# A hybrid attention block in fp32r on one core: the rooms of weights moved 64 bytes up in SBUF

## The chip, the core and the metric

The kernel runs on one core of one Trainium2 chip. The metric is the device time of one execution in microseconds; of several runs the median is given. A profile is one further execution, recorded by the hardware profiler. Its span reaches from the first to the last recorded instruction; the time of a run holds a few microseconds more around it.

## What is computed

One layer of a decoder block over 512 tokens and 16 learned meta tokens (L = 528), width 1024, in float32:

```python
u = rmsnorm(h, pre_norm_g)                      # h: 528 x 1024
proj = u @ w_in                                 # 1024 x 7600
cq, ckv, k_pe, z_mla, fq, fk, fv, f, z_fox, gate_a, gate_b = split(proj)
q = (rmsnorm(cq) @ w_uq)                        # 16 heads, 64 plain + 32 rotary columns
k_nope, v_mla = (rmsnorm(ckv) @ w_ukv)
o_mla = causal_attention(q, k, v_mla)
o_fox = causal_attention(fq, fk, fv, cum=cumsum(log_sigmoid(f + b)))
y_mla = (o_mla * silu(z_mla)) @ w_br_mla
y_fox = (o_fox * silu(z_fox)) @ w_br_fox
mixed = (sigmoid(gate_a) * y_mla + sigmoid(gate_b) * y_fox) @ w_out
out = (h + rmsnorm(mixed, post_norm_g))[16:]
```

## The kernel before

Every product is made of matmuls of 128 rows by 128 columns of weights against up to 512 columns of tokens. To keep float32's precision each operand is split into a high and a low part (tile names ending in h and l), and a product is three matmuls: high by high, high by low, low by high. So one unit of work, 128 output columns of `w_in`, is 8 blocks of the inner dimension times 3, that is 24 matmuls, all issued by `mm` (line 98).

**Where the operands lie.** A matmul has a stationary operand, which is loaded into the array ahead of it (the profile's PEld, one load for each matmul), and a moving operand, which streams through. In `unit` (matmuls from `mm`, line 98) the weights are stationary and the tokens are moving. The rooms are:
- `uTh`, `uTl`: the normalised tokens, 8 blocks of 576 columns (2304 bytes) each. The meta tokens stand in columns 48 to 63 of a block and the real tokens from column 64 on, so that real tokens begin at a multiple of 256 bytes.
- the pool `wp`, three rooms each of `wraw` (weights as they come from DRAM), `wh` and `wl` (their high and low parts), 4096 bytes a room. At the start its `wraw` rooms also hold three tiles of x.
- `cTh`, `cTl`: the latent tokens, three blocks of 528 columns (2112 bytes).
- in the last stage `gh`, `gl` (the gated attention outputs), `a1h`, `a1l`, `a2h`, `a2l` (sums and halves of the merged branches) and again the rooms of `uTh`, `uTl`, reused for sums.

**The stages.** First the tokens are normalised and turned, with the small projections (`psm`). Then come 16 stages of attention, FoX and MLA in turn for each of 8 pairs of heads; each has its scores (`st`) and its values (`ov`), and between them, to fill the wait for softmax, the units of the next stage: `fq`, `fk`, `v`, `z` against `uTh`/`uTl`, and `mq`, `mk`, `v` and `ppe` against `cTh`/`cTl`. A product over all 528 tokens (`fk`, `v`, `mk`) is cut into 272 columns, which begin at the meta tokens, and 256 columns. Then the gates (`pg`) and the two branch products follow: one by a fast scheme of seven half products over 256 columns for each of four pairs of blocks (`pair_py`: tiles `x`, `y`, `z`), the other plainly (`py`, 512 columns). Last comes `w_out`, where the weights move and the tokens are stationary (`x`, `y`, `z` again).

**What sets the order.** PE's order is the order of the code (`manual_schedule`). ScalarE makes `wh` from `wraw` (line 131), GpSimd or VectorE makes `wl` (line 104). All DMAs are issued by SyncE's queue. The loads of the next three units are issued when a unit begins (`ahead`), and each waits until its `wraw` room is free.

**What sets the addresses.** A pool takes its rooms from the bottom of SBUF upward in the order in which pools and tiles are opened, or, with side="right", from the top downward. `const`, with `ident`, `eps_t`, `uTh` and `uTl`, lies at the bottom, `wp` follows it, and what is opened later lies above `wp`: in the attention `cqk` (with `cTh`, `cTl`) and the rest, in the last stage, when `cqk` is closed, `gh`, `gl` and others directly above `wp`. `a1h` to `a2l`, `tb`, `gT` and `th` lie on the right side.

Of the kernel before, what the change touches and what calls it, by code (L numbers as in the profile page):

```python
# [11 lines left out]
F32 = mybir.dt.float32  # L12
# [43 lines left out]
def block_kernel(ctx: ExitStack, tc: tile.TileContext, x, meta_tokens, pre_norm_g, w_in, fox_forget_b,  # L56
# [11 lines left out]
    const = ctx.enter_context(tc.tile_pool(name="const", bufs=1))  # L68
# [6 lines left out]
    nc.gpsimd.memset(eps_t[:, 1:2], 4.0 * EPS)  # L75
    uT0 = [const.tile([128, KD, ROW + L - META], F32R, tag=n, name=n) for n in ("uTh", "uTl")]
    uTh, uTl = (t[:, :, ROW - META :] for t in uT0)
    padp = ctx.enter_context(tc.tile_pool(name="padp", bufs=1, side="right"))
    pad = padp.tile([128, 56], F32, tag="pad", name="pad")

# [84 lines left out]
    thp = ctx.enter_context(tc.tile_pool(name="thp", bufs=5, side="right"))  # L165
    cctx = ExitStack()
    cqk = cctx.enter_context(tc.tile_pool(name="cqk", bufs=1))
    cTh = cqk.tile([128, 3, L], F32R, tag="cTh", name="cTh")
    cTl = cqk.tile([128, 3, L], F32R, tag="cTl", name="cTl")
    accp = ctx.enter_context(tc.tile_pool(name="accp", bufs=3, space=PSUM))  # L170
# [1223 lines left out]
```

## Time and profile before

| | us |
|---|---|
| three runs: median (lowest, highest) | 587.31 (587.02, 587.46) |
| span of the profiled execution | 584.6 |
| PE busy | 575.7 (98%) |
| PEld, the loads of stationary operands | 496.8 (85%) |
| VectorE busy | 416.4 (71%) |
| ScalarE busy | 357.4 (61%) |
| GpSimd busy | 199.4 (34%) |
| DMA, share of 16 engines | 70.3% |

The profile gives no time of its own for the profiled execution beside its span. The span lies 2.7 us below the median of the runs, which is what lies around it if that execution was an average one.

How to read it: a PE busy time of 98% says only that matmuls overlap without a gap, since a matmul's record reaches from its start to its modelled end, and the next one starts long before that. How fast PE really goes is read from the distance between the starts of two matmuls, called the pitch here: in the chain of work that ended last a piece "5.44 PE z L98 x24" means that 24 matmuls took 5.44 us from the first start to the start of what followed, a pitch of 226.7 ns. In a group's row the second number behind the bar is the mean record of one matmul, so two groups of the same width with records 7 ns apart have pitches about 7 ns apart.

### The profile page before, as it was taken

To read this page: it belongs to the slowest core of one execution; us is meant where nothing else is said; L and a number is where in the kernel's file an instruction comes from. 1 tells how busy PE (TensorE), PEld (TensorE's weight loads), DVE (VectorE), ACT (ScalarE), POOL (GpSimd) and SP (SyncE) were. 2 spreads that over 40 slices of the span, in tenths; PEclk is the share of its full clock that TensorE was granted. 3 is DMA by queue.
4 is the path that set the end of the run, shared out by engine and by line. 5 is a ranking of instruction groups with operands and counts; after the bars stand their busy time and mean duration, and the time that the engine had idled before them with its cause. 6 is when DMAs were issued, how large, how long until landed. Compare 5 with 4: busy or idle time off the path is not lost.

```text
span 584.6 us, 11115 instructions
## 1 busy us (share of the span) xinstructions
PE 575.7 (98%) x3841; PEld 496.8 (85%) x3841; DVE 416.4 (71%) x1156; ACT 357.4 (61%) x816; POOL 199.4 (34%) x270
## 2 busy tenths in 40 slices
PE   8999999999999999999999999999999999999996
PEld 6989889889889888888898898878998998888884
DVE  5854877885776775767758748896647876468966
ACT  7856774893774775767748747944343462443762
POOL 4317745464468462654554634510000000000000
PEclk9999999999999999999999999999999999999998
DMA  8535599989977999988986976977722534233503
GB/s 295 122 83 163 127 176 230 231 195 248 177 167 158 228 191 206 219 172 207 183 176 180 219 154 147 183 172 236 233 73 72 145 104 144 78 109 108 217 0 144
DMA packets 220000, 97.47 MB, mean 167 GB/s; under 512 B 131456, under 2 KB 209672, under 8 KB 219944
## 3 DMA queue, kind: packets, MB, share of 16 engines
q1 hardware_dynamic: 219944, 96.77, 70.3%
q8 instruction: 30, 0.49, 0.3%
q14 instruction: 26, 0.21, 0.1%
HBM read 62.36 MB, written 3.97 MB: 113 GB/s over the span
## 4 chain that ended last, share of the span: by engine, by line
PE 96%; ACT 1%; DMA 1%; issue 0%; SPq 0%; DVE 0%; POOL 0%; DVEq 0%; ACTq 0%; POOLq 0%
PE z L98 19%; PE pg L98 15%; PE v L98 9%; PE fk L98 8%; PE st L98 8%; PE fq L98 8%; PE x L98 8%; PE py L98 7%; PE ov L98 5%; PE psm L98 3%; PE y L98 2%; PE mq L98 2%; PE mk L98 1%; PE ppe L98 1%; DMA wsr<-in_w_in_dram 1%; ACT uTh L371 0%
## 5 line engine op out<-in xcount | busy, mean ns | idle before, releaser
L104 POOL TENSOR_TENSOR wl<-wraw,wh 128x1024 fp32r<-128x1024 f32 (+2 forms) x61 | 118.3, 1947 | 112.2 <-ACT wh L131 80.5
L131 ACT CAST wh<-wraw 128x1024 fp32r<-128x1024 f32 (+1 forms) x72 | 74.6, 1042 | 56.4 <-PE py L98 16.8
L826 ACT ACTIVATE sf<-sf,nb 128x272 f32<-128x272 f32 (+3 forms) x128 | 72.7, 569 | 11.5 <-DVE nb L791 10.6
L865 DVE SCALAR_TENSOR_TENSOR pn<-sf,ri,pn 128x512 f16<-128x512 f32 (+3 forms) x128 | 69.6, 609 | 1.6 <-ACT pn L861 1.5
L104 DVE TENSOR_TENSOR wl<-wraw,wh 128x512 fp32r<-128x512 f32 (+1 forms) x55 | 52.2, 950 | 23.9 <-ACT wh L1119 17.8
L861 ACT ACTIVATE pn<-sf,ri 128x128 f16<-128x128 f32 (+3 forms) x128 | 59.7, 548 | 0.5 <-DVE ri L831 0.5
L98 PE MATMUL z<-uTh,wh 128*128 128x512 f32 x128 | 50.9, 398 | 0.0
L98 PE MATMUL pg<-uTh,wh 128*128 128x512 f32 x128 | 50.2, 392 | 0.0
L98 PE MATMUL z<-uTl,wh 128*128 128x512 f32 x128 | 50.1, 391 | 0.0
L98 PE MATMUL z<-uTh,wl 128*128 128x512 f32 x128 | 50.0, 390 | 0.0
L98 PE MATMUL pg<-uTl,wh 128*128 128x512 f32 x128 | 49.9, 390 | 0.0
L98 PE MATMUL pg<-uTh,wl 128*128 128x512 f32 x128 | 49.8, 389 | 0.0
L706 DVE TENSOR_REDUCE vsc<-v 128x1 f32<-128x272 f32 (+1 forms) x32 | 13.2, 433 | 39.8 <-PE v L98 39.8
L98 PE MATMUL st<-hlk,hlq 64*128 64x272 f32 (+4 forms) x480 | 41.3, 299 | 0.0
L1119 ACT CAST wh<-wraw 128x512 fp32r<-128x512 f32 x28 | 17.3, 618 | 37.9 <-DVE wraw L1128 17.0
L98 PE MATMUL v<-uTh,wl 128*128 128x256 f32 (+1 forms) x128 | 36.5, 285 | 0.0
L98 PE MATMUL fk<-uTl,wh 128*128 128x256 f32 (+1 forms) x128 | 36.4, 285 | 0.0
L98 PEld LDWEIGHTS st<-hlk,hlq 64*128 64x128 f32 x480 | 33.0, 186 | 4.1 <-ACT vh L725 2.8
L98 PE MATMUL fk<-uTh,wh 128*128 128x256 f32 (+1 forms) x128 | 36.4, 285 | 0.0
L98 PE MATMUL v<-uTl,wh 128*128 128x256 f32 (+1 forms) x128 | 36.4, 285 | 0.0
L98 PE MATMUL fk<-uTh,wl 128*128 128x256 f32 (+1 forms) x128 | 36.4, 285 | 0.0
L98 PE MATMUL v<-uTh,wh 128*128 128x256 f32 (+1 forms) x128 | 36.4, 284 | 0.0
(295 smaller groups left out, 1612.3 us busy)
## 6 DMA issues: line engine op xcount, KB each, us to landing
wraw<-in_w_in_dram SPq DMA_DIRECT2D x56, 512.0 KB, 4.8
cbp<-c_dram SPq DMA_DIRECT2D x16, 264.0 KB, 4.1
wraw<-in_w_br_fox_dram SPq DMA_DIRECT2D x8, 512.0 KB, 4.5
tb<-in_w_out_dram SPq DMA_DIRECT2D x8, 512.0 KB, 5.4
wraw<-in_w_br_mla_dram SPq DMA_DIRECT2D x8, 512.0 KB, 4.3
wraw<-in_w_out_dram SPq DMA_DIRECT2D x6, 512.0 KB, 3.6
xr<-in_x_dram SPq DMA_DIRECT2D x4, 512.0 KB
out_dram<-yo SPq DMA_DIRECT2D x8, 256.0 KB, 2.0
```

Source lines behind the costliest of these rows:

```text
L98: nc.tensor.matmul(*a, **k)
L104: return eng.tensor_tensor(out=lo, in0=src, in1=f32(hi), op=ALU.subtract)
L131: nc.scalar.copy(wh[:, :n], raw[:, :n])
L706: nc.vector.tensor_reduce(out=sc[:, i : i + 1], in_=ps, op=ALU.max, axis=AX.X, apply_absolute_value=True)
L826: exps[b // 3] = nc.scalar.activation(sf, sf, AF.Exp, bias=sums["nb"][:, h, b : b + 1], scale=-1.0, accum_out=sums["su"][:, h, b : b + 1]).ins
L861: normed[:] = [nc.scalar.activation(hi, sf, AF.Copy, scale=rib).ins]
L865: nc.vector.scalar_tensor_tensor(out=lo, in0=sf, scalar=rib, in1=hi, op0=ALU.mult, op1=ALU.subtract)
L1119: nc.scalar.copy(to[0], src)
```

## The change

Two tiles that nothing reads or writes are put between the others. The first is 16 float32 (64 bytes for each partition) at the end of `const`; it moves all that lies above it on that side by 64 bytes. The second is 48 float32 (192 bytes) at the start of `cqk`; it moves `cTh`, `cTl` and what is opened behind them by 192 bytes more, 256 in all.

```diff
@@ -75,6 +75,7 @@
     uT0 = [const.tile([128, KD, ROW + L - META], F32R, tag=n, name=n) for n in ("uTh", "uTl")]
     uTh, uTl = (t[:, :, ROW - META :] for t in uT0)
+    const.tile([128, 16], F32, tag="shift", name="shift")
     padp = ctx.enter_context(tc.tile_pool(name="padp", bufs=1, side="right"))
@@ -165,6 +166,7 @@
     cctx = ExitStack()
     cqk = cctx.enter_context(tc.tile_pool(name="cqk", bufs=1))
+    cqk.tile([128, 48], F32, tag="shift", name="shift2")
     cTh = cqk.tile([128, 3, L], F32R, tag="cTh", name="cTh")
```

The instructions, their order on each engine and their waits are the same in both kernels; only addresses differ. They are, for the first byte of each room:

| room | before | after | modulo 256 before, after |
|---|---|---|---|
| `uTh`, `uTl` (real tokens begin 256 bytes later) | 17152, 35584 | the same | 0, 0 |
| `wraw`, three rooms | 54016, 58112, 62208 | +64 | 0, 64 |
| `wh`, three rooms | 66304, 70400, 74496 | +64 | 0, 64 |
| `wl`, three rooms | 78592, 82688, 86784 | +64 | 0, 64 |
| `cTh`, `cTl` and all else of the attention on this side | 90880, 97216 | +256 | unchanged |
| `gh`, `gl`, and in the last stage also `thx`, `yo`, `xr`, `gp` | 90880, 107264 | +64 | 0, 64 |
| `a1h`, `a1l`, `a2h`, `a2l`, `tb` | 161216, 165312, 169408, 177600, from 128448 on | the same | 192, 192 |

A block of weights is 128 columns, 512 bytes, so all blocks of a `wh` room share the room's remainder. What matmuls meet, as remainders modulo 256 of the moving and the stationary operand's first byte:

| matmuls | count | columns | before | after |
|---|---|---|---|---|
| `z`, `pg`, `fq` against `uTh`, `uTl` | 960 | 512 | 0, 0 | 0, 64 |
| `fk`, `v`, second part | 384 | 256 | 0, 0 | 0, 64 |
| `fk`, `v`, first part (begins at the meta tokens) | 384 | 272 | 192, 0 | 192, 64 |
| `py` (512 columns), and `x`, `y`, `z` of `pair_py` against `gh`, `gl` (256) | 192 + 192 | 512, 256 | 0, 0 | 64, 64 |
| `x`, `z` of `pair_py` against `a1h` to `a2l` | 144 | 256 | 192, 0 | 192, 64 |
| `w_out`, `x` and `z` with the rooms of `uTh`, `uTl` stationary | 96 | 512 | 0, 0 | 64, 0 |
| `w_out`, `x` and `y` with `a1h` to `a2l` stationary | 48 | 512 | 0, 192 | 64, 192 |
| `mq`, `ppe`, `mk`, MLA's `v` against `cTh`, `cTl` | 168 | 512, 272, 256 | 0 to 192, 0 | 0 to 192, 64 |
| scores, values, `psm`, transposes, the last 24 of `w_out` | the rest | | unchanged | unchanged |

## The prediction

> **What bounds the kernel now.** I read the page first: busy shares, clock and the chain that ended last.
>
> ```profile
> span 584.6 us, 11115 instructions
> PE 575.7 (98%) x3841; PEld 496.8 (85%) x3841; DVE 416.4 (71%) x1156; ACT 357.4 (61%) x816; POOL 199.4 (34%) x270
> PEclk9999999999999999999999999999999999999998
> PE 96%; ACT 1%; DMA 1%; issue 0%; SPq 0%; DVE 0%; POOL 0%; DVEq 0%; ACTq 0%; POOLq 0%
> ```
>
> PE holds 96% of the chain, at full clock. No weights are waited for in the body: DMA's 1% is one load at the start. So the time is the number of matmuls times their pitch, and since the change adds, removes and moves no instruction, only a change of pitch, or a weight load that becomes late, can reach the end. I went on to the chain in order of time, which gives pitches of stretches without a wait.
>
> ```profile
> 430.78 1.44 PE z L98 x12
> 436.40 1.36 PE z L98 x12
> 546.02 5.49 PE y L98 x24
> 551.51 5.44 PE z L98 x24
> ```
>
> The columns are start, length, what, and how many matmuls. The first two are twelve matmuls of 256 columns each, in the same scheme: 1.44/12 = 120.0 ns against 1.36/12 = 113.3 ns. They differ in the moving operand alone: `gh` and `gl` (remainder 0 modulo 256) in the first, `a2h` and `a2l` (192) in the second, with weights at 0 in both. The last two are 24 of 512 columns in `w_out`: 5.49/24 = 228.8 ns with stationary `a2h`, `a2l` (192), 5.44/24 = 226.7 ns with the rooms of `uTh`, `uTl` (0), moving weights at 0 in both. So **the place of the operands modulo 256 goes with the pitch**, by up to 6.7 ns a matmul, and in both directions. I call "distance" the stationary remainder less the moving one, modulo 256: 0 gives 120.0 and 226.7, 64 gives 113.3, 192 gives 228.8. That distance and not the two places decides is an assumption; the rows don't hold all pairs of places.
>
> [...]
>
> **The change part by part.** 1. *Long matmuls against the tokens*: `z`, `pg`, `fq`, from places 0, 0 to 0, 64.
>
> ```profile
> L98 PE MATMUL z<-uTh,wh 128*128 128x512 f32 x128 | 50.9, 398 | 0.0
> L98 PE MATMUL pg<-uTh,wh 128*128 128x512 f32 x128 | 50.2, 392 | 0.0
> L98 PE MATMUL fq<-uTh,wh 128*128 128x512 f32 x64 | 25.9, 405 | 0.0
> 174.17 2.80 PE ppe L98 x12
> 497.00 5.44 PE pg L98 x24
> 567.83 10.99 PE x L98 x48
> ```
>
> Each of these three groups has two sisters (tokens low, weights low) of the same count: 3 x (128 + 128 + 64) = 960 matmuls, at 5.44/24 = 226.7 ns in an undisturbed stretch of `pg`. The trace shows no long matmul at distance 64. The long ones at mixed or other distances are `y` above (228.8), `ppe` (2.80/12 = 233.3, latent tokens at 0, 64 and 128) and the last 48 `x` (10.99/48 = 229.0; half of them run at 0, half with `a2h`, `a2l`). None of these is under 226.7, so for 512 columns the present place looks like the floor. I take the mean of the three rows, (5.49 + 10.99 + 2.80)/84 = 229.5 ns: 960 x (229.5 - 226.7) = **+2.7 us**. Ends: 233.3 gives 960 x 6.6 = +6.3; nothing excludes that distance 64 helps here as it does at 256 columns, 960 x (-6.7) = -6.4.
>
> 2. *Second parts of `fk` and `v`*, 256 columns, from 0, 0 to 0, 64.
>
> ```profile
> L98 PE MATMUL fk<-uTh,wh 128*128 128x256 f32 x64 | 18.1, 283 | 0.0
> L98 PE MATMUL z<-a2h,wh 128*128 128x256 f32 x16 | 4.4, 276 | 0.0
> L98 PE MATMUL mk<-cTl,wh 128*128 128x256 f32 x8 | 2.3, 283 | 0.0
> ```
>
> Six such groups of 64 (two tensors, three passes) are 384 matmuls at a record of 283 ns, that is 120.0 ns of pitch. At distance 64 stands the second row, 276 ns, or 113.3 of pitch. I take it: 384 x (-6.7) = **-2.6 us**. Ends: -2.6, and 0 if places count and not the distance; a loss is bounded by the step from `z` to `mk` in the other direction, +2.6.
>
> 3. *First parts of `fk` and `v`*, 272 columns, distance 64 to 128.
>
> ```profile
> L98 PE MATMUL fk<-uTh,wl 128*128 128x272 f32 x64 | 18.3, 287 | 0.0
> L98 PE MATMUL v<-cTh,wl 128*128 128x272 f32 x8 | 2.3, 288 | 0.0
> L98 PE MATMUL mk<-cTl,wh 128*128 128x272 f32 x8 | 2.4, 294 | 0.0
> ```
>
> Again 384. `cTh`'s third block begins at remainder 128, so the second row has distance 128: 1 ns more, **+0.4 us**. Ends: 0, and the third row's +7 ns, +2.7.
>
> 4. *`pair_py` against `a1h` to `a2l`*, 144 of 256 columns, distance 64 to 128. `mk` with `cTl` in part 2's rows has distance 128 and 283 ns against 276: 144 x 6.7 = **+1.0 us**, ends 0 and +1.0.
>
> 5. *`py` and `pair_py` against `gh`, `gl`*: both operands move, distance stays 0, so **0**. Upper end by the pair of rows with both at 192 against both at 0:
>
> ```profile
> L98 PE MATMUL x<-a1h,a2h 128*128 128x512 f32 x4 | 1.6, 394 | 0.0
> L98 PE MATMUL py<-gh,wh 128*128 128x512 f32 x64 | 24.9, 389 | 0.0
> ```
>
> 5 ns for 384 matmuls, +1.9; a gain of the size of part 2 would be 192 x 6.7 = -1.3.
>
> 6. *`w_out`*: 96 go from distance 0 to 192, at 228.8 instead of 226.7: **+0.2 us**; 48 go from 192 to 128, taken as 0; ends -0.3 and +0.9 (233.3 for all 144). *Latent tokens*, 168: their distances are permuted, **0**, ends 168 x 3 ns = 0.5 to either side.
>
> 7. *The DMAs and the other engines* work on rooms 64 bytes higher.
>
> ```profile
> GB/s 224 331 297 341 399 405 405 405 397 389 328 347 316 302 248 31 6 3 151 345 172 162 334 143 0 0 0 0 0 0 0 0 0 0 0 20 177 333 213 290
> GB/s 0 0 0 0 0 0 0 0 0 0 0 37 53 328 406 225 33 37 369 393 213 4 0 0 0 0 57 29 328 406 225 4 0 139 279 229 205 279 385 410
> wraw<-in_w_in_dram SPq DMA_DIRECT2D x56, 512.0 KB, 4.8
> L131 ACT CAST wh<-wraw 128x1024 fp32r<-128x1024 f32 x70 | 73.5, 1053 | 56.4 <-PE py L98 16.8 <-PE v L98 11.7 <-PE z L98 7.2
> L131 ACT CAST wh<-tb 128x1024 fp32r<-128x1024 f32 x6 | 6.3, 1045 | 1.7 <-PE z L98 1.2 <-PE x L98 0.5
> ```
>
> The first row is the window 404 to 436 us, where `w_out` is loaded into `tb` at remainder 192; the second is 525 to 545 us, the same rows of 2048 bytes into `wraw` at 0. Both reach about 405 GB/s, so the remainder costs those DMAs nothing. ScalarE's cast takes 1045 ns from `tb` and 1053 from `wraw`. I cost all this at **0**; the cover is the load's lead: 4.8 us from issue to landing for weights that 24 matmuls of 226.7 ns (5.4 us) use up, with three units loaded ahead. Were that cover gone, each of some 70 units would wait for what the load exceeds 5.4 us by.
>
> [...]
>
> **Sum**: 2.7 - 2.6 + 0.4 + 1.0 + 0 + 0.2 + 0 = +1.7 us on the profiled execution, whose span of 584.6 lies 2.7 under the runs' median of 587.31, a difference that I carry over: 587.31 + 1.7 = **589.0 us**.
>
> **The rivals.** *A: the long matmuls gain too.* If distance 64 saves 512 columns what it saves 256, part 1 is -6.4 and the sum 2.7 + 6.4 = 9.1 lower: -7.4 us, 579.9; half of it, 583.1. The price is 0.96 us for each ns of the long pitch; the other parts sum to -1.0, so this rival decides as soon as the long pitch falls by 0.2 ns. For it: 113.3 against 120.0. Against it: no long row below 226.7.
>
> [...]
>
> *C: the odd place of the weights costs everywhere.* Long at 233.3 as `ppe`, +6.3, and part 2 without its gain, 0: 6.3 + 0 + 0.4 + 1.0 + 0.2 = +7.9, 595.2; with the gain +5.3, 592.6. For it: `ppe`, the one stretch whose moving operand is off the multiple of 256 with weights at 0. Against it: `y` and `x` at 229.
>
> *D: weights come late.* If the landing went from 4.8 to over 5.4 us by 0.3, 70 units would give +21 us, 608. Against it: the two GB/s rows.
>
> **How the numbers follow.** The forecast has 0.33, A 0.20, B 0.22, C 0.23, D 0.02. The forecast's own range is 588.4 to 591. The range for 8 in 10 leaves out the far half of A and the top of C with D: **583.0 to 594.5**. What a measurement can tell from no change is about 0.2%, 1.2 us: faster (below 586.1) is A, 0.20, and a little of B, 0.02; same is B, 0.20, and the forecast's low end, 0.05; slower the rest: **0.22, 0.25, 0.53**.
>
> **What would show it.** In the chain of the changed kernel: a stretch of 24 `pg` or `z` that took 5.44 us takes 5.51 (A: 5.28 or 5.36; B: 5.44; C: 5.60). `fk` and `v` second parts have records of 276 ns (C: 283). `x` and `z` against `a1h` to `a2l` take 1.44 us for twelve and not 1.36. `y` and `z` of `w_out` both take 5.49. Landings stay near 4.8 us, and PE waits for no weights; D would put DMA into the chain. The forecast is wrong if the distance doesn't carry from 256 to 512 columns as I assume it doesn't, or if the place of one operand alone sets the pitch.

## The result and the profile after

The changed kernel takes **592.69 us** (median; runs from 592.2 to 593.53) against 587.28 beside it: a ratio of 1.0086, 95% interval 1.0067 to 1.0105, so +5.4 us. The forecast was 589.0 and the range 583.0 to 594.5, with slower by over 0.2% as the likeliest side. Side and range held; the mechanism did too, but the largest term had been put at about half of what was measured.

The page of the changed kernel, the lines that answer to those shown of before (`mm` is now line 99):

```profile
span 591.4 us, 11115 instructions
PE 580.7 (98%) x3841; PEld 496.8 (84%) x3841; DVE 414.7 (70%) x1156; ACT 357.1 (60%) x816; POOL 200.1 (34%) x270
PE 95%; DMA 2%; ACT 1%; issue 0%; SPq 0%; DVE 0%; POOL 0%; DVEq 0%; ACTq 0%; POOLq 0%
```

PE still holds the chain with the same 3841 matmuls, at a granted clock of 0.998 over the span (0.997 in the profile before). The profiled execution was the slowest of the four runs (593.53; span 591.4, which is 6.8 over before's). DMA's share of the chain went from 1 to 2%: some of the 6.8 us is no matmul's.

The chain of work that ended last, in order of time (start, length, what, how many matmuls):

```profile
217.98 3.04 PE fk L99 x24
...
226.79 2.72 PE fk L99 x24
...
422.87 11.21 PE pg L99 x48
...
441.23 1.43 PE z L99 x12
...
552.47 5.58 PE y L99 x24
558.04 5.50 PE z L99 x24
```

The same stage of before reads, in its chain:

```profile
215.05 2.96 PE fk L98 x24
...
223.84 2.88 PE fk L98 x24
226.72 2.19 PE st L98 x30
...
418.44 10.91 PE pg L98 x48
```

The first parts of `fk` (272 columns) went from 2.96 to 3.04 us, 123.3 to 126.7 ns a matmul. The second parts (256 columns) went from 2.88 to 2.72, 120.0 to 113.3: the gain that the prediction saw. But 48 `pg` went from 10.91 to 11.21, that is from 227.3 to 233.5 ns, where 229.5 was forecast. In `pair_py` the piece `z` against `a2h`, `a2l` went from 1.36 (at 436.40 before) to 1.43. In `w_out`, `y` rose to 5.58 (232.5 ns, distance 128) and `z` to 5.50 (229.2, distance 192).

The groups say the same (the second number behind the bar is the mean record in ns):

```profile
L99 PE MATMUL z<-uTh,wh 128*128 128x512 f32 x128 | 51.4, 402 | 0.0
L99 PE MATMUL pg<-uTh,wh 128*128 128x512 f32 x128 | 50.9, 397 | 0.0
L99 PE MATMUL py<-gh,wh 128*128 128x512 f32 x64 | 24.9, 389 | 0.0
L99 PE MATMUL fk<-uTh,wh 128*128 128x256 f32 x64 | 17.7, 276 | 0.0
```

Before, these records were 398, 392, 389 and 283 ns. `py`, where both operands moved by 64, stands still.

What of the 6.8 us isn't pitch shows in two other views of the changed kernel: the DMAs (the last number is the median us from issue to landing), and what PE waited for (us in total, times, longest).

```profile
wraw<-in_w_in_dram SPq DMA_DIRECT2D x56, 512.0 KB, 5.3
```

```profile
PE psm L99 <- POOL wsh L304: 1.7, 1, 1.7
PE ov L99 <- DMA pt<-pn: 0.8, 1, 0.8
```

The loads of `w_in` into `wraw` land 5.3 us after issue instead of 4.8, PE waited 1.7 us at the start (1.0 before), and once 0.8 us for a transpose of probabilities, a DMA that SyncE issues as it does the loads. The same view has one more wait of `ov`, 0.4 us, put down to `st`.

Adding up the times from each matmul's start to the next one's in both traces, by kind, gives the balance beside the prediction's terms:

| term | predicted | measured, us |
|---|---|---|
| 1. `z`, `pg`, `fq`, 512 columns | +2.7 | +5.0 |
| 2. second parts, 256 columns | -2.6 | -2.4 |
| 3. first parts, 272 columns | +0.4 | +1.3 |
| 4. `pair_py` against `a1h` to `a2l` | +1.0 | +0.7 |
| 5. `py`, `gh`, `gl` | 0 | +0.1 |
| 6. `w_out`; latent tokens | +0.2; 0 | +0.4; -0.45 |
| 7. DMAs | 0 | 2.1 outside the terms above, in this execution |

### The profile page after: what moved, and what is told of

It reads as the page before. It is cut to its first block, busy times and chain, and to the rows that moved or that the text cites. A ratio compares the mean times of both kernels' runs of the same rounds, so it can differ in the third digit from the quotient of the medians.

```text
span 591.4 us, 11115 instructions
## 1 busy us (share of the span) xinstructions
PE 580.7 (98%) x3841; PEld 496.8 (84%) x3841; DVE 414.7 (70%) x1156; ACT 357.1 (60%) x816; POOL 200.1 (34%) x270
## 4 chain that ended last, share of the span: by engine, by line
PE 95%; DMA 2%; ACT 1%; issue 0%; SPq 0%; DVE 0%; POOL 0%; DVEq 0%; ACTq 0%; POOLq 0%
PE z L99 19%; PE pg L99 15%; PE v L99 9%; PE fq L99 8%; PE x L99 8%; PE fk L99 7%; PE py L99 7%; PE st L99 7%; PE ov L99 5%; PE psm L99 3%; PE y L99 2%; PE mq L99 2%; PE mk L99 1%; PE ppe L99 1%; DMA wsr<-in_w_in_dram 1%; DMA pt<-pn 1%
## 5 line engine op out<-in xcount | busy, mean ns | idle before, releaser
L105 POOL TENSOR_TENSOR wl<-wraw,wh 128x1024 fp32r<-128x1024 f32 (+2 forms) x61 | 118.2, 1945 | 115.4 <-ACT wh L132 85.6
```

Source lines behind the costliest of these rows:

```text
L105: return eng.tensor_tensor(out=lo, in0=src, in1=f32(hi), op=ALU.subtract)
```

## The experiments

Three theories were put against each other. **Distance**: the pitch goes by the stationary remainder less the moving one, modulo 256, and by the number of columns. **Place of the weights**: weights off a multiple of 256 cost, wherever the tokens lie (the prediction's rival C). **Loads**: what costs is DMA into rooms at 64. All times are medians beside a median of the kernel before on the same chip.

| run | time | before | ratio | 95% |
|---|---|---|---|---|
| e1_tokens_too | 588.48 | 587.35 | 1.0020 | 1.0011 to 1.0030 |
| e2_raw_only | 588.01 | 587.35 | 1.0012 | 1.0002 to 1.0021 |
| e3_hilo_only | 591.49 | 587.35 | 1.0069 | 1.0055 to 1.0082 |
| e4_by_128 | 593.98 | 587.35 | 1.0111 | 1.0095 to 1.0127 |
| e5_by_192 | 591.65 | 587.23 | 1.0075 | 1.0062 to 1.0088 |
| e6_fk_256_first | 592.74 | 587.23 | 1.0093 | 1.0079 to 1.0107 |
| e7_fk_and_gh | 592.35 | 587.23 | 1.0087 | 1.0073 to 1.0101 |
| e8_by_32 | 593.16 | 587.23 | 1.0102 | 1.0088 to 1.0115 |
| e9_by_256 | 586.84 | 587.08 | 1.0001 | 0.9992 to 1.0010 |
| e10_fk_v_up | 594.11 | 587.08 | 1.0118 | 1.0102 to 1.0134 |
| e11_fk_v_up_kept | 586.02 | 587.17 | 0.9985 | 0.9973 to 0.9997 |
| e12_rooms_only | 587.14 | 587.17 | 1.0000 | 0.9992 to 1.0009 |

### e1: tokens and weights both 64 bytes up

```diff
+    const.tile([128, 16], F32, tag="shift", name="shift")
     uT0 = [const.tile([128, KD, ROW + L - META], F32R, tag=n, name=n) for n in ("uTh", "uTl")]
     uTh, uTl = (t[:, :, ROW - META :] for t in uT0)
-    const.tile([128, 16], F32, tag="shift", name="shift")
```

> The 64 bytes are put ahead of the rooms of the normalised tokens, so that tokens and weights both lie 64 bytes higher; the raw rooms too. Distance (stationary less moving remainder modulo 256 sets the pitch): the 960 long matmuls are back at distance 0 and 226.7 ns, fk and v back at 123.3 and 120.0; what stays is pair_py against the halves at 192, 144 x 6.7 ns = +1.0 us, and 48 of w_out at distance 128, +0.2, and the loads' share, 0 to 1 us: 588.3 to 589.5. Place of the weights alone (weights at 64 cost wherever the tokens lie): long stay at 233.3, time stays at 592 to 593. Loads (rows of 512 bytes into raw rooms at 64 are what costs): also 592 to 593, but with the long pitch at 226.7.

588.48. Its chain, the same places as above:

```profile
216.28 2.96 PE fk L99 x24
...
225.07 2.88 PE fk L99 x24
...
419.68 10.91 PE pg L99 x48
...
437.74 1.43 PE z L99 x12
```

These three pitches are back to before's, 227.3, 123.3 and 120.0, with the weights still at 64. What doesn't come back is `pair_py` against `a1h` to `a2l`, which no edit moved and whose distance stays 128: its `z` takes 1.43 us, as in the changed kernel. So the place of the weights costs nothing by itself, and rival C's reason falls: the pitch goes with the distance. The time lies in the range that was expected from distance.

### e2 and e3: raw rooms alone, high and low parts alone

In e2 the 16 columns stand at the start of `wp` and 48 more behind the raw rooms; in e3 16 columns stand behind the raw rooms, and the 48 at the start of `cqk` stay. The edit of e2:

```diff
     wp = ctx.enter_context(tc.tile_pool(name="wp", bufs=3))
+    wp.tile([128, 16], F32, tag="shift", name="shift", bufs=1)
...
         load_h(0)
+        wp.tile([128, 48], F32, tag="shift2", name="shift2", bufs=1)
```

> Only the raw rooms lie 64 bytes higher, the high and low parts and gh, gl are back at multiples of 256, so no operand of a matmul has moved in its remainder. Distance, and place of the weights: all pitches as before, time 587.3 plus what the longer loads cost, 0 to 1.5 us, so 587.3 to 588.8, with landings of 5.3 us instead of 4.8. Loads as the whole cause: 592 to 593.

> The raw rooms are back in their place, the high and low parts and gh, gl stay 64 bytes higher. Distance, and place of the weights: all matmuls as in the changed kernel, long at 233.3, so +4 to +5 us: 591.3 to 592.3; the rest up to 592.7 is the loads' share. Landings are back at 4.8 us. Loads as the whole cause: 587.3 to 588.

588.01 and 591.49: +0.7 and +4.1 us, together 4.8 of the change's 5.4, and both where distance expected them. The DMA view of e2, and what PE waited for there:

```profile
wraw<-in_w_in_dram SPq DMA_DIRECT2D x56, 512.0 KB, 5.2
```

```profile
PE ov L99 <- DMA pt<-pn: 0.3, 1, 0.3
```

The chain of e3, and its DMA view:

```profile
421.19 11.21 PE pg L98 x48
```

```profile
wraw<-in_w_in_dram SPq DMA_DIRECT2D x56, 512.0 KB, 4.7
```

The longer landing goes with the raw rooms, the longer pitch with the high and low parts: the times between starts give terms 1 to 4 in e3 as +5.0, -2.4, +1.2 and +0.7 again, and in e2 each as 0.0. Of the loads' price of 0.7 us (interval 0.1 to 1.2) the profile of e2 shows small waits of `ov` in the first stages, never a wait for weights. Such waits, for `pt` and put down to `st`, add up to 1.2 us in the changed kernel, 1.0 in e1 and 0.6 in e2, whose raw rooms stand at 64, and to 0 to 0.2 in before, e3, e6, e9, e10, e11 and e12, whose raw rooms stand at 0. The wait at the start doesn't part the runs so: 0.9 to 1.7 us against 0.2 to 1.0. How far off the raw rooms stand doesn't show in the landings: the runs e8, e4 and e5 below, at 32, 128 and 192 bytes, have 5.2 us for `w_in`, as e2 has at 64; e1 has 5.3. Nor does every load land later: those of `w_br_fox` went from 4.5 us in before to 5.1 in the changed kernel and 5.0 in e2, those of `w_br_mla` from 4.3 to 4.3 and 3.9.

### e4, e5, e8, e9: other distances

The first pad of the change is 32, 48, 8 and 64 columns instead of 16, the second 32, 16, 56 and none.

> All rooms of weights 128 bytes higher instead of 64. Distance: long at distance 128, which y of w_out shows at 232.5 ns, 960 x 5.8 = +5.6, less a fifth for the slow first matmuls of a stretch that are slow anyway, +4.5; fk and v second parts at 128, 119.3 ns, -0.3; first parts at 192, not seen yet, 126.7 to 130, +1.3 to +2.6; pair_py against the halves at 192, between 118 and 120, +0.7 to +1.0; w_out +0.8; loads 0 to 1: 594.5 to 597, slower than at 64. Place of the weights alone, any place off a multiple of 256 costing the same: 592 to 593.

> All rooms of weights 192 bytes higher. Distance: long at 192, where w_out before has 228.8 ns, 960 x 2.1 = +2.0; fk and v first parts (192, 192) at distance 0, not seen at 272 columns, 123 to 127, so 0 to +1.3; second parts at 192, not seen at 256 columns, 118 to 120, -0.8 to 0; pair_py against the halves at distance 0, 144 x 6.7 = +1.0; w_out 96 at distance 64, 233.3, +0.6; raw rooms off their place +0.7 as measured alone: 590.5 to 593, likeliest 591.5, faster than by 64 and by 128. Place of the weights alone, any place off a multiple of 256 costing the same: 592 to 594.

> All rooms of weights 32 bytes higher, a distance that no run has shown. If the pitch follows distance in steps of 64 bytes, 32 is like 0 or like 64, and the time is 587.3 to 588.5 or 592 to 593; between them if the pitch goes evenly. If another remainder suits 512 columns better than 0, as 64 suits 256 better than 0, long fall by up to 6.7 ns, 960 x -6.7 = -6.4, and the time goes down to 581. Raw rooms off their place +0.7 in each.

> All rooms of weights 256 bytes higher, the same remainders modulo 256 as before, raw rooms included. Distance with a period of 256: all pitches as before, 226.7 for long, 120.0 for second parts; 587.3, at most 0.3 off. If the period is longer (512 or more), or if any move costs, whatever the remainder: another pitch for the long matmuls, 960 x 2 to 6.7 ns, so 589 or more, or less than 587.

Rows of the four chains: `fk`'s first and second part, then 48 `pg`. By 128 bytes (e4):

```profile
217.44 3.04 PE fk L99 x24
...
226.35 2.85 PE fk L99 x24
...
422.97 11.16 PE pg L99 x48
```

By 192 bytes (e5):

```profile
217.67 3.01 PE fk L99 x24
...
226.50 2.82 PE fk L99 x24
...
442.91 11.20 PE pg L99 x48
...
551.23 5.44 PE y L99 x24
556.67 5.60 PE z L99 x24
```

By 32 bytes (e8):

```profile
217.21 2.96 PE fk L99 x24
...
225.97 2.84 PE fk L99 x24
...
422.54 11.19 PE pg L99 x48
```

By 256 bytes (e9):

```profile
215.02 2.96 PE fk L99 x24
...
223.82 2.88 PE fk L99 x24
...
418.41 10.91 PE pg L99 x48
```

With 256 bytes all is as before (586.84), so moving costs nothing in itself, and the pitches come back after 256 bytes, though not after 32, 64, 128 or 192. For 512 columns distance 0 is the best place of those tried (10.91 us for 48 `pg`), and 32, 64 and 128 (11.19, 11.21 and 11.16 us) lie within 1.1 ns a matmul of one another at the top. The expectation for 128 had the right signs and was 0.5 us too high at its low end. For 192 the median fell inside its range, though `pg` stood at 233.3 and not at 228.8 in this stretch; the starts in the trace give 229.0 for `fq`, `z` and five of nine stretches of `pg`, 233.3 for the other four. The two rows of `w_out` in e5 test distance once more: their stationary rooms didn't move, and with the moving weights at 192 `y` (192, distance 0) falls from 228.8 to 226.7 ns, while `z` (0, distance 64) rises from 226.7 to 233.3. For 32 both outcomes had been allowed, and the time is 0.2 us above the upper one; it is like 64 for 512 columns, but without the full gain of the second parts (118.2).

### e6 and e7: move the tokens' start instead, and gh, gl

e6 cuts `fk` into 256 columns and then 272, so that both parts begin at remainder 192. e7 adds to that a place 48 columns up, `gx`, from which `pair_py` reads what it read from `gh`, `gl`.

```diff
-        return unit(f"fk{pr}", win_w(O_FK, pr), u_act, KD, ALLT, hl_done(("k", 1, pr), L, HALF), keybank[0])
+        return unit(f"fk{pr}", win_w(O_FK, pr), u_act, KD, [slice(0, 256), slice(256, L)], hl_done(("k", 1, pr), L, 256), keybank[0])
...
-            w_ = min(w, n - o)
+            w_ = ps.shape[1]
```

```diff
-        gh, gl = (m2.tile([128, KD, S], F32R, tag=n, name=n) for n in ("gh", "gl"))
+        g0 = [m2.tile([128, KD * S + 64], F32R, tag=n, name=n) for n in ("gh", "gl")]
+        gh, gl = (t[:, 0 : KD * S].rearrange("p (k s) -> p k s", k=KD) for t in g0)
+        gx = [t[:, 48 : 48 + KD * S].rearrange("p (k s) -> p k s", k=KD) for t in g0]
```

> No address moves. fk is cut into 256 columns first, beginning at the meta tokens (remainder 192), and 272 columns then, which so begin at remainder 192 too, in place of 272 and then 256 at 0. Distance: both parts now stand at distance 64, 123.3 + 113.3 instead of 123.3 + 120.0 ns: 192 x -6.7 = -1.3 us, 586.0. Place of the weights alone, or no effect of the moving operand's place: 587.3, and all second parts keep 120.

> As the one with fk cut 256 first, and gh, gl stand 48 columns (192 bytes) further in their tile during pair_py, and at the tile's start again for py. Distance: the 192 matmuls of pair_py against gh, gl go from distance 0 to 64, 120.0 to 113.3 ns, another -1.3 us: 584.7, less than both kernels. Place of the weights alone: 587.3.

592.74 and 592.35: both expectations failed. The chain of e6, where before has 2.96, 2.88 and then 2.19 for 30 `st`:

```profile
217.60 2.83 PE fk L98 x24
220.43 5.83 PE v L98 x48
226.26 2.99 PE fk L98 x24
...
229.27 0.40 ACT hlk L247
...
229.71 2.48 PE st L98 x30
```

Two things show. The scores of the second block of queries need keys up to column 272, and with the cut at 256 those come from the late part, so PE waits 0.46 us for ScalarE's `hlk`, and the 30 `st` behind the stop take 2.48 us instead of 2.19: 0.75 for this stage. Seven of the eight stages have such a stop. By the times between starts the part of 272 columns, stops included, takes 4.5 us more over the whole trace than in before, the `st` 1.5 more and the part of 256 columns 1.1 less, which covers the loss. And the first part runs at 2.83/24 = 117.9 ns, not at the 113.3 of distance 64. All pairs in e7's chain show that pitch:

```profile
436.45 1.41 PE z L98 x12
...
442.10 1.41 PE z L98 x12
```

The starts give 353.3 ns for three, or 117.8 each. The first `z` is the stretch against `gx`, the second the one against `a2h`, whose address no edit touched and which has 1.36 in the kernel before. **So 256 columns at distance 64 have two steady pitches, 113.3 and 117.8**, and which one comes goes with what ran ahead. In e6 the stretch that follows 24 `fq` at 226.7 directly has 117.8 in seven of eight stages; in the changed kernel it follows a first part at 126.7 and has 113.3 in all. In before the stretches at distance 64 in `pair_py` follow ones at 120.0, or one another; in e7 the first follows `pg` at 226.7, no stretch of the pair differs from the one ahead, and the pitch stays as it came. No run varied what runs ahead and nothing else, and what sets the choice inside PE isn't shown.

### e10, e11, e12: the gain without the loss

If distance is right, 64 bytes up for the weights of `fk` and `v` alone keeps terms 2 and 3 and drops the rest. e10 has rooms of 1088 columns for the attention, closed and opened anew at 1024 for the last stage. e11 keeps the long rooms throughout; the space comes from one room of the gates and the place of the post-norm gain. e12 is e11 with no weights moved up. The edit of e11, the move itself:

```diff
-        wh, wl = (wp.tile([128, 1024], F32R, tag=t, name=f"{t}{u}") for t in ("wh", "wl"))
+        wh, wl = (wp.tile([128, 1088], F32R, tag=t, name=f"{t}{u}") for t in ("wh", "wl"))
+        wh, wl = wh[:, up:], wl[:, up:]
...
-        return unit(f"fk{pr}", win_w(O_FK, pr), u_act, KD, ALLT, hl_done(("k", 1, pr), L, HALF), keybank[0])
+        return unit(f"fk{pr}", win_w(O_FK, pr, 16), u_act, KD, ALLT, hl_done(("k", 1, pr), L, HALF), keybank[0])
...
-                get, nk, act = win_w(O_FV, pr), KD, u_act
+                get, nk, act = win_w(O_FV, pr, 16), KD, u_act
```

> Rooms of high and low parts are 1088 columns long in the attention, and the weights of fk and v alone stand 16 columns (64 bytes) up in them; all else has its remainder of before, raw rooms too. Distance: the gain of the changed kernel without its loss, fk and v second parts 113.3, first parts 126.7, long 226.7: its rows give -2.4 + 1.2 = -1.2 us: 586.1, faster than both kernels. Distance with a memory (the pitch that a stretch of 256 columns takes depends on what ran ahead of it, as 117.8 in place of 113.3 after stretches at 226.7 suggests): here both 256 parts come behind first parts at 126.7, as in the changed kernel, so again 113.3 and 586.1; with 117.8 it would be 384 x 4.5 = 1.7 more, 587.8.

> The weights of fk and v alone 64 bytes up, as in the run before, but the rooms of 1088 columns stay through the last stage, so none is opened anew there and no unit waits for one; to make space, one room of the gates in the last stage is given up (six are needed at once, seven were there) and the post-norm gain lies in two gate rooms. Distance, with the pitches that the run before showed (113.3 and 126.7, long 226.7): -1.2 us, 586.0 to 586.2, and without the wait of 7 us at the first gate of the last stage. If the rest of the run before's loss was not that wait: 588 or more.

> The same rooms of 1088 columns and the same gate rooms, but no weights moved up in them: all remainders modulo 256 as before. Distance: 587.3, all pitches as before; what it differs from that is the price of the other rooms, to be taken off the run beside it.

e10: 594.11. Its chain has the pitches that were expected, and a gap where the last stage begins:

```profile
214.56 3.04 PE fk L100 x24
...
223.37 2.72 PE fk L100 x24
...
393.71 2.96 PE pg L100 x12
...
396.69 0.60 ACT th L546
397.29 0.94 ACT gh L1124
...
400.61 1.15 DVE wl L106
...
401.80 7.34 PE pg L100 x22
```

```profile
PEclk9999999999999999999999999997999999999999
```

From the end of 12 `pg` at 396.67 (393.71 + 2.96) to 401.80 PE is short of weights and starts only two matmuls: in the chain the split for the first gate of the last stage (`wl`) stands behind ScalarE's and VectorE's work on `th`, `gh` and `gl`, where the kernel before has no stop. A second loss comes with the stop, in the second fence: the slice from 399 to 414 us has 7 tenths of the full clock (the whole execution 0.993, that of e11 0.998). Behind the stop the granted clock is 0.50 from 401.80 to 406.00, and nine matmuls of 512 columns start 427 ns apart instead of 226.7. By the times between starts `pg` takes 7.0 us more in all, 4.9 of it in the stop. The expectation had counted pitches and not what reopened rooms do to the lead of the weights. e11, whose rooms stay, has no such gap: 586.02, ratio 0.9985 (0.9973 to 0.9997), 1.15 us under the kernel before and some 6.7 under the changed one. Its chain:

```profile
215.04 3.04 PE fk L98 x24
...
223.85 2.72 PE fk L98 x24
...
417.84 10.91 PE pg L98 x48
```

Short parts as in the changed kernel, long ones as before. e12, at 587.14, shows that the rooms alone change nothing, so the 1.15 us are the distance's; the starts in e11's own trace give -2.4 for term 2 and +1.2 for term 3, 1.2 less in sum. The interval ends at 0.9997: the gain is small, but there, and by its median this version beats both kernels (its runs reach from 585.38 to 588.43).

## Why the prediction was right, and where not

**That the pitch would move, by distance** (the assumption of the first part): right. e1 brings the pitches back with the weights at 64, e5 does the same with both operands at 192, e9 brings all back after 256 bytes (48 `pg` in 10.91 us), and `py` (term 5) stood still. The pitch is not all: the loads (term 7) have some 0.7 us of the 5.4. That the place counts at all is plainest in 48 `pg`, the same instructions from other places: 10.91 us before and 11.21 after.

**Term 1, the long matmuls**: the direction was right and the size wrong, +5.0 instead of +2.7. This is the step that failed. The steady pitch at distance 64 is 233.3 ns, and the prediction took 229.5, a mean over three rows that stand at other distances (`y` and half of `x` at 192, `ppe` at several). The other distances give 228.8 to 233.3 each for itself; their mean is the pitch of none. 233.3 stood there as the upper end, +6.3; the rest down to 5.0 is that the first matmuls of a stretch were slow already before (the second to the seventh 228.4 to 233.0 ns in the mean). The mark that the prediction gave to rival C, 24 `pg` in 5.60 us, is what the trace shows, and C with the gain of the second parts, 592.6, is where the time fell. C's reason, however, is refuted by e1.

**Term 2, second parts**: right to 0.2 us, because the trace of before held that very width at that very distance. The second pitch of 117.8 for the same pair, met in e6 and e7, didn't come into play; nothing in the prediction excluded it, so the close hit has some luck in it.

**Term 3, first parts**: 3.3 ns a matmul (123.3 to 126.7) instead of 1, so +1.3 and not +0.4. The row used was from the same distance, but of 8 matmuls in short stretches.

**Term 4** was +0.7 for +1.0: these stretches are 12 long, and the first matmuls of each were slow in before as well. **Terms 5 and 6** were nearly right; the 48 of `w_out` that go from 192 to 128 were taken as 0 and went from 228.8 to 232.5 ns.

**Term 7, the DMAs at 0**: too low by 0.7 us in the median, by e2 (interval 0.1 to 1.2), and landings didn't stay near 4.8 us but went to 5.3. The cover named there, the lead of the loads, held, since no unit waited for weights. Not named was that `ov` would wait for the first transposes of probabilities. Of the 2.1 us outside the terms in the profiled execution some 1.3 are waits of `ov` in the first stages; most of the rest is at the start, and no run shows that it comes of the raw rooms.

**Rival B** (that next to nothing happens, to which 0.22 was given) and **rival A** (long ones gain too) fall with the same row of 48 `pg`: A had carried a gain from 256 to 512 columns without a row at that width. **Rival D** didn't occur.

The sum from single parts, 0.7 by the raw rooms and 4.1 by the high and low parts, is 4.8 of 5.4; the 0.6 between lies within the intervals and isn't explained further.

## What to carry to other kernels

Where PE is the bound and its matmuls run without a gap, read the pitch by width and by the operands' distance modulo 256 before rooms are moved, and keep long stretches at the distance that shows the lowest pitch; a width at a distance that the trace doesn't hold has a pitch of its own, which no mean of others gives (here 233.3 ns at 512 columns, not 229.5). A shift that helps one width can cost another (here 113.3 ns for 120.0 at 256 columns, 233.3 for 226.7 at 512), so move the operand of those units alone. And a saving in pitch is lost at once where a cut puts a wait of half a microsecond into each stage (e6), or a room's release one stop of 5 us into the last (e10).

## What the runs showed of the hardware

Steady pitches in ns, by columns and distance, from the starts of matmuls in these traces (128 rows by 128 columns stationary):

| columns | 0 | 32 | 64 | 96 | 128 | 192 |
|---|---|---|---|---|---|---|
| 512 | 226.7 | 233.3 | 233.3 | not run | 232.5 | 229.0 or 233.3 |
| 272 | 125.5 | not run | 123.3 | 123.5 | 126.6 | 126.6 |
| 256 | 120.0 | 118.2 | 113.3 or 117.8 | 117.6 | 118.7 | 117.8 |

At 0 they are from before, for 272 columns from e5; at 32 and 96 from e8, for 256 columns at 96 from stretches of 12 matmuls alone; at 64 from the changed kernel, for 272 columns from before, the 117.8 from e6 and e7; at 128 from the changed kernel and e4; at 192 from before and e5, for 272 columns from e4. The first matmuls of a stretch differ from these pitches: in before the first seven of 22 stretches of `z`, `pg` and `fq` took 307, 233.0, 229.2, 233.0, 229.7, 228.8 and 228.4 ns in the mean, those behind them 226.5 to 226.9.

Not expected were that the best distance differs by width (0 for 512 columns, 64 for 272 and 256), that some pairs have two steady pitches with a choice that goes with the stretch ahead and is kept to the end of the stretch (256 columns at 64: 113.3 behind 126.7, 117.8 behind 226.7), and that the steps between pitches are often 6.7 or 3.3 ns (120.0 to 113.3, 123.3 to 126.6). The loads of `w_in`, 512 KB in rows of 512 bytes, into rooms at 32, 64, 128 and 192 bytes above a multiple of 256 landed in 5.2 to 5.3 us, whichever of them it was, instead of 4.8 in before and 4.7 in e3. And behind a stop of PE of 5 us the granted clock stood at 0.50 for at least 4.2 us (e10).
